# State layer of an encoder block: input weights turned in 64x64 corners, shifted inputs laid by transfers

## The chip, the cores and the metric

The kernel runs on one core of a Trainium2 chip. The metric is the device time of one execution in microseconds (us). Five engines run side by side, each with its own queue worked in order: TensorE (PE in the profile; its weight loads are PEld), VectorE (DVE), ScalarE (ACT), GpSimd (POOL) and SyncE (SP), which here issues nearly all DMA transfers. They wait for each other through semaphores.

## The reference, cut to what matters

One layer of an encoder: 256 tokens of width 2048, all in float32. A normalised input goes through one projection whose columns feed three groups of heads; their outputs are normalised, joined, projected and added to the input; an MLP follows. The change touches the second group, the state layer:

```python
lam_bar = jnp.exp(lam * dt)                       # per group (32) and state (64), complex
b_bar = ((lam_bar - 1.0) / lam)[..., None] * b    # (group, state 64, channel 16)
bu = jnp.einsum('bsgc,gpc->bsgp', u, b_bar)       # what each token puts into each state
a = jnp.broadcast_to(lam_bar, bu.shape)
_, h = lax.associative_scan(combine, (a, bu), axis=1, reverse=reverse)   # x_t = a x_(t-1) + bu_t
y = jnp.einsum('bsgp,gcp->bsgc', h, c).real       # forward and backward, own parameters
```

There are 32 groups of 16 channels, and two directions.

## The kernel before

**The weight stream.** All large weights (209 MB read in all) come as 372 transfers of one stream, `A["w"]`, in the order in which they are used: chunks of 128 x 1024 floats, 512 KB each. `w_dma` issues a chunk on SP into one of three buffers `wraw`. `conv_high` has ACT round it to a shorter format (`wh`), `conv_low` has DVE form the rest (`wl`), three buffers each. `take` hands PE 128 columns at a time; every product is made of three matmuls (high x high, high x low, low x high). When PE comes to chunk c, chunk c + 2 is converted, and after that conversion chunk c + 5 is issued. Chunks 0 to 15 are the first projection columns; 16 to 31 project the memory tokens: a chunk there is 12 matmuls with the weights held (`mem_k`), then 6 with the weights streamed (`mem_v`).

**Tasks between.** All other work is written as Python generators (tasks). `tick`, called twice a chunk, advances them; a rough clock of each engine (`clk`, costs in `Engine.__getattr__`) decides when a task is due. That happens while the program is built: what comes out is one fixed list of instructions per engine. A task's PE work therefore stands at a fixed place among the weight matmuls, and where its inputs are late, all of PE waits.

**The state layer.** Four tokens are taken together as a block (64 blocks, `NB`), 8 groups make a tile `ut` (4 tiles). `prep_b(ut)` has DVE form b_bar times the powers 0 to 3 of lam_bar in `W`, each power from the one before through `pt`. Two groups lie in the 128 partitions of W (states of group j in partitions 64j to 64j + 63). For the products with the inputs, channels have to lie in the partitions: ACT copies W into the zeroed tile `wx`, where group j's 64 columns (4 powers of 16 channels) lie between those of the other group, so that the two don't mix; PE transposes eight 128 x 128 pieces per direction; ACT moves them from PSUM into `W1T`. One `wx` serves both directions in turn.

`U4` holds the layer's input for this: token i of each block in partitions 32i to 32i + 31, so that one matmul sums over four tokens. It is made from `uT` (channels in partitions, blocks along the row) by 16 copies in `g0_evac`, eight each on ACT and POOL. `incr(ut, d)` multiplies: 32 matmuls of 128 rows by 32 columns, four strips of columns of the array side by side. ACT moves the result to `XS`; `tree` scans it on DVE, and `ssm_out` multiplies with c.

In the profile nearly all instructions carry L155, the helper that records an operation, so tiles tell them apart; `U4` is shown as U.

Of the kernel before, what the change touches and what calls it, by code (L numbers as in the profile page):

```python
# [11 lines left out]
F32 = mybir.dt.float32  # L12
# [15 lines left out]
MEMH = 4  # L28
EPS = 1e-6
LAM_RE_MAX = -1e-4  # L30
NB = S // 4
LEV = 6
SCALE = 128 ** -0.5
# [70 lines left out]
def hybrid_kernel(ctx: ExitStack, tc: tile.TileContext, A: dict, out: bass.AP, dbg=None):  # L104
    nc = tc.nc
    ctx.enter_context(tc.manual_schedule())
    mult, add, sub = ALU.mult, ALU.add, ALU.subtract
# [13 lines left out]
    class Engine:  # L121
# [3 lines left out]
        def __getattr__(self, name):  # L125
            f = getattr(self.raw, name)
            e = self.e

            def call(o, *a, **kw):
                n = 1  # L130
                for d in o.shape[1:]:
                    n *= d
                if e == "E":
                    m = a[0].shape[-1]
                    if name == "transpose":
                        c = 110.0
                    elif a[0].dtype == F32R:
                        c = n * 0.4225
                    else:
                        c = max(n, 128) * 1.69 * (0.31 if m == 32 else 1.0) if n > 4 else 110.0  # L140
                elif name == "tensor_reduce":
                    c = 80 + 1.04 * a[0].shape[1] * a[0].shape[2]
                elif e == "A":
                    c = (205 + 0.83 * n + (80 if isinstance(kw.get("scale"), bass.AP) or "bias" in kw else 0)
                         + (186 if "accum_out" in kw else 0))
                elif e == "V":
                    c = (72 if n > 64 else 140) + n * {"tensor_copy": 0.52, "reciprocal": 8.0, "tensor_tensor_scan": 1.04,
                                   "tensor_scalar": 0.76, "memset": 0.3}.get(name, 1.04)
                else:
                    c = 155 + n * {"tensor_scalar": 0.9, "memset": 0.0, "tensor_copy": 1.6}.get(name, 2.1)  # L150
                if e == "V" and n > 64 and name == "tensor_tensor" and any(
                        abs(x.ap[-1][0]) >= 4 for x in (o, a[0]) if x.ap[-1][1] > 1):
                    c += 0.9 * n
                book(e, c)
                return f(o, *a, **kw)  # L155
            return call

    V, G, ACT, PE = (Engine(e, r) for e, r in zip("VGAE", (nc.vector, nc.gpsimd, nc.scalar, nc.tensor)))
# [9 lines left out]
    def att():  # L168
        return ps.tile([128, 512], F32, name="att", tag="bank", bufs=6)
# [4 lines left out]
    def tt(eng, o, a, b, op):  # L174
        eng.tensor_tensor(o, a, b, op=op)
# [10 lines left out]
    def act(o, i, f=AF.Copy, **kw):  # L186
        ACT.activation(o, i, f, **kw)
# [28 lines left out]
    ident = const.tile([128, 128], F32, name="ident")  # L216
# [59 lines left out]
    def after(ns):  # L276
        t = clk["E"] + ns
        while clk["E"] < t:
            yield
# [5 lines left out]
    def done(e):  # L285

        t = clk[e] + MARGIN
        while clk["E"] < t:
            yield
# [11 lines left out]
    class W:  # L301
        raw = {}
# [139 lines left out]
    a2 = A2.enter_context(tc.tile_pool(name="a2", bufs=1, side="right"))  # L442
# [58 lines left out]
    for k in range(KT):  # L501
        c = k if k < 2 else 1 + k // 2
# [149 lines left out]
    W0, CC, XS = {}, {}, {}  # L652
# [5 lines left out]
    uT = a2.tile([128, 4, 256], F32, name="uT")  # L658
    U4 = a2.tile([128, 16, NB], F32, name="U4")

    wx = a2.tile([128, 8, 4, 2, 16], F32, name="wx")
    V.memset(wx.rearrange("p n l j b -> p (n l j b)"), 0.0)

    loaded = {}

    def load_b(ut):
# [5 lines left out]
    def prep_b(ut):  # L672
        yield from until(lambda: ut in loaded and clk["E"] > loaded[ut][1])
        raw = loaded[ut][0]
        w = a2.tile([128, 2, 2, 4, 4, 16], F32, name="W", tag="W", bufs=1)
        par = a2.tile([128, 4, 2, 2, 4], F32, name="par", tag="par", bufs=1)
        for i, x in enumerate((cfr, cfi, lbr, lbi)):
            act(par[:, i], x[:, 8 * ut:8 * ut + 8].rearrange("p (d q) -> p d q", d=2)[:, :, None, :]
                .to_broadcast([128, 2, 2, 4]))
        yield from done("A")  # L680
        for l in range(4):
            o = w[:, :, :, :, l, :]
            src = (w[:, :, :, :, l - 1, :].rearrange("p d c q b -> p (d c q) b") if l
                   else raw.rearrange("p (n b) -> p n b", b=16))
            r_, i_ = (par[:, 2 * min(l, 1) + i].rearrange("p d c q -> p (d c q)")[:, :, None].to_broadcast([128, 16, 16])
                      for i in range(2))
            t = a2.tile([128, 2, 2, 4, 16], F32, name="pt", tag="pt", bufs=1)
            tt(V, t.rearrange("p d c q b -> p (d c q) b"), src, i_, mult)
            tt(V, o.rearrange("p d c q b -> p (d c q) b"), src, r_, mult)
            tt(V, o[:, :, 0], o[:, :, 0], t[:, :, 1], sub)  # L690
            tt(V, o[:, :, 1], o[:, :, 1], t[:, :, 0], add)
            yield True
        yield from done("V")
        act(W0[ut].rearrange("p d c q j b -> p (d c q) j b"),
            w[:, :, :, :, 0, :].rearrange("p d c q b -> p (d c q) b")[:, :, None, :].to_broadcast([128, 16, 2, 16]))
        w0_done.add(ut)
        if ut % 2 == 0:
            XS[ut // 2] = a2.tile([128, 2, 16, NB], F32, name="XS", tag="AB", bufs=2)
        for d in range(2):
            for j in range(2):  # L700
                h = slice(64 * j, 64 * j + 64)
                act(wx[h, :, ::-1 if d == 0 else 1, j, :], w[h, d].rearrange("p c q l b -> p (c q) l b"))
            yield PE
            wt = a2.tile([128, 2, 4, 128], F32, name="W1T", tag="W1T", bufs=2)
            ps2 = [att(), att()]
            for n in range(8):
                PE.transpose(ps2[n // 4][:, n % 4 * 128:(n % 4 + 1) * 128], wx[:, n].rearrange("p l j b -> p (l j b)"),
                             ident)
            for c in range(2):
                act(wt[:, c].rearrange("p q m -> p (q m)"), ps2[c])  # L710
            spawn(incr(ut, d, wt, clk["A"] + MARGIN + LAG[2]), 2, "A")
            yield True

    def incr(ut, d, wt, t0):

        yield from until(lambda: ssm_done and clk["E"] > t0 and (d == 0 or (ut, 0) in xs_part))
        p = att()
        X = p.rearrange("p (c q m) -> p c q m", c=2, q=4)
        for c in range(2):
            for q in range(4):  # L720
                for m in range(4):
                    PE.matmul(X[32 * m:32 * m + 32, c, q, :], wt[:, c, q, 32 * m:32 * m + 32], U4[:, 4 * ut + q, :],
                              start=True, stop=True, skip_group_check=True, tile_position=(0, 32 * m))
        c0 = 8 * (ut % 2) + 4 * d
        act(XS[ut // 2][:, :, c0:c0 + 4, ::-1 if d else 1], X)
        xs_part.add((ut, d))
        yield
# [251 lines left out]
    def g0_evac():  # L979
        b = st_rx["b"]  # L980
        for j in range(2):
            tt(V, qkm[:, 2 * j:2 * j + 2, 0, :], pq[j].rearrange("p (a b) -> p a b", a=2),
               b[:, None, :].to_broadcast([128, 2, 256]), mult)
        yield
        for u in range(4):
            tt(V, uT[:, u].rearrange("p (r c) -> p c r", c=16),
               pu[:, u * 256:(u + 1) * 256].rearrange("p (c r) -> p c r", c=16), b.rearrange("p (c r) -> p c r", c=16),
               mult)
        yield
        for q in range(4):  # L990
            for i in range(4):
                o = U4[32 * i:32 * i + 32, q:16:4, :]
                s = uT[32 * q:32 * q + 32, :, i * NB:(i + 1) * NB]
                if i % 2:
                    G.tensor_copy(o, s)
                else:
                    act(o, s)
            if q < 3:
                yield True
        ssm_done.append(1)  # L1000
        if dbg:
            dbg("uT", uT.rearrange("p a b -> p (a b)"))
        yield
# [64 lines left out]
    for g in range(2):  # L1068
        pv2 = [acc(), acc()]
        for k in range(KT):  # L1070
            wh, wl = take(4)
            for t in range(2):
                s = slice(t * 128, (t + 1) * 128)
# [4 lines left out]
        for h in range(4 * g, 4 * g + 4):  # L1078
            load_bias(h)
            pp = acc()  # L1080
            for j in range(2):
                for k in range(KT):
# [4 lines left out]
                        stop=(k == KT - 1))  # L1087
# [137 lines left out]
    pt = []  # L1225
# [10 lines left out]
    for t, c, _ in parts:  # L1236
        p = acc()
        s = slice(t * 128, (t + 1) * 128)
        b = slice(c.start - 1536, c.stop - 1536)
# [121 lines left out]
    def x1_task():  # L1361
        for o in range(4):
            for t in range(2):
# [8 lines left out]
    rt, r22, r24, vb, v, y, tn, r = (small.tile([128, 2], F32, name=n, bufs=1)  # L1372
                                 for n in ("rt2", "r22", "r24", "vb", "fv", "fy", "ft", "fr2"))
# [28 lines left out]
    for half in range(2):  # L1402
# [19 lines left out]
        for o in range(4):  # L1422
# [18 lines left out]
            c = slice(o * 512, (o + 1) * 512)  # L1441
# [102 lines left out]
```

## Time and profile before

| | us |
|---|---|
| median of 3 runs | 1140.99 (1138.22 to 1141.76) |
| the profiled execution | 1140.01 |
| its span, first to last instruction | 1138.2 |
| PE busy | 1111.2 (98%) |
| DVE busy | 721.3 (63%) |
| ACT busy | 578.3 (51%) |
| POOL busy | 104.8 (9%) |
| mean rate of DMA | 187 GB/s |

Busy time of PE is modelled at the matmuls' ends, so gaps count where they are shown. A row of groups gives the line, the engine, the operation, what is written and read, and the number; a row of a timeline begins with its start and its length in us. A row of stretches gives, after the stretch's length, the busy time of PE, PEld, DVE, ACT and POOL, then the clock granted to TensorE (1.00 is full), the share of the DMA engines and GB/s.

### The profile page before, as it was taken

To read this page: it belongs to the slowest core of one execution; us is meant where nothing else is said; L and a number is where in the kernel's file an instruction comes from. 1 tells how busy PE (TensorE), PEld (TensorE's weight loads), DVE (VectorE), ACT (ScalarE), POOL (GpSimd) and SP (SyncE) were. 2 spreads that over 40 slices of the span, in tenths; PEclk is the share of its full clock that TensorE was granted. 3 is DMA by queue.
4 is the path that set the end of the run, shared out by engine and by line. 5 is a ranking of instruction groups with operands and counts; after the bars stand their busy time and mean duration, and the time that the engine had idled before them with its cause. 6 is when DMAs were issued, how large, how long until landed. Compare 5 with 4: busy or idle time off the path is not lost.

```text
span 1138.2 us, 18307 instructions
## 1 busy us (share of the span) xinstructions
PE 1111.2 (98%) x7208; PEld 957.6 (84%) x7208; DVE 721.3 (63%) x1069; ACT 578.3 (51%) x900; POOL 104.8 (9%) x179
## 2 busy tenths in 40 slices
PE   8999999899999999999999999999999999999996
PEld 8988899799788878888888888888888888888885
DVE  6777588888876776866664444445666665445454
ACT  6567856636655464644455434434444444344341
POOL 1780000020110161000000000000000000001010
PEclk9999999999999999999999999999999999999999
DMA  9876444345455766666666666666666666666663
GB/s 302 291 254 184 127 145 142 114 140 166 135 148 179 249 188 181 189 191 191 187 186 193 189 189 186 186 187 192 193 186 189 191 191 187 186 198 195 193 209 129
DMA packets 62726, 212.31 MB, mean 187 GB/s; under 512 B 7216, under 2 KB 9776, under 8 KB 62640
## 3 DMA queue, kind: packets, MB, share of 16 engines
q1 hardware_dynamic: 62352, 211.05, 60.5%
q8 instruction: 56, 0.92, 0.3%
q14 instruction: 30, 0.25, 0.1%
q10 hardware_dynamic: 288, 0.09, 0.0%
HBM read 209.02 MB, written 2.10 MB: 185 GB/s over the span
## 4 chain that ended last, share of the span: by engine, by line
PE 83%; DVE 7%; DMA 3%; ACT 3%; issue 2%; POOL 1%; SPq 0%; DVEq 0%; POOLq 0%; ACTq 0%
PE acc L155 74%; PE big L155 6%; PE att L155 4%; DMA wraw<-in_w_dram 3%; DVE wl L155 3%; ACT wh L155 1%; DVE ps L155 1%; DVE W L155 1%; DVE XS L155 1%; ACT P L155 0%; DVE pt L155 0%; DVE mn L155 0%; DVE P L155 0%; POOL x L155 0%; DMA gpost<-in_post_dram 0%
## 5 line engine op out<-in xcount | busy, mean ns | idle before, releaser
L155 DVE TENSOR_TENSOR wl<-wraw,wh 128x1024 fp32r<-128x1024 f32 (+1 forms) x372 | 458.3, 1234 | 374.9 <-ACT wh L155 374.3
L155 ACT ACTIVATE wh<-wraw 128x1024 fp32r<-128x1024 f32 (+1 forms) x372 | 391.4, 1054 | 440.5 <-PE acc L155 275.3
L155 PE MATMUL acc<-hs,wh 128*128 128x512 f32 (+1 forms) x996 | 345.9, 391 | 0.0
L155 PE MATMUL acc<-hs,wl 128*128 128x256 f32 x992 | 279.3, 282 | 0.0
L155 PEld LDWEIGHTS acc<-hs,wh 128*128 128x128 f32 x996 | 186.6, 188 | 38.8 <-ACT hs L155 0.2
L155 PEld LDWEIGHTS acc<-hs,wl 128*128 128x128 f32 x992 | 187.3, 189 | 0.0
L155 PE MATMUL acc<-wh,fH 128*128 128x512 f32 x448 | 178.7, 399 | 0.0
L155 PE MATMUL acc<-wh,fL 128*128 128x512 f32 x448 | 176.5, 394 | 0.0
L155 PE MATMUL acc<-wl,fH 128*128 128x512 f32 x448 | 175.7, 392 | 0.0
L155 PEld LDWEIGHTS acc<-wh,fL 128*128 128x128 f32 x448 | 84.1, 188 | 22.0
L155 PEld LDWEIGHTS acc<-wl,fH 128*128 128x128 f32 x448 | 84.1, 188 | 19.9
L155 PEld LDWEIGHTS acc<-wh,fH 128*128 128x128 f32 x448 | 84.1, 188 | 19.4
L155 PE MATMUL acc<-xH,wh 128*128 128x256 f32 x256 | 74.4, 291 | 0.0
L155 PE MATMUL acc<-xH,wl 128*128 128x256 f32 x256 | 72.0, 281 | 1.4 <-DVE wl L155 1.4
L155 PE MATMUL acc<-xL,wh 128*128 128x256 f32 x256 | 71.9, 281 | 0.2 <-issue 0.2
L155 POOL TENSOR_TENSOR facc<-facc,g 128x512 f32<-128x512 f32 x6 | 9.3, 1572 | 474.8 <-DMA g<-in_g_dram 474.8
L155 PEld LDWEIGHTS acc<-xH,wl 128*128 128x128 f32 x256 | 48.3, 188 | 1.9 <-DVE wl L155 1.6
L155 PEld LDWEIGHTS acc<-xH,wh 128*128 128x128 f32 x256 | 48.3, 189 | 0.8
L155 PEld LDWEIGHTS acc<-xL,wh 128*128 128x128 f32 x256 | 48.4, 189 | 0.1
L155 PE MATMUL acc<-wh,mixn 128*128 128x512 f32 x128 | 41.0, 398 | 0.0
L155 ACT ACTIVATE P<-P,mn 128x160 f32<-128x160 f32 (+1 forms) x24 | 10.8, 449 | 46.0 <-DVE mn L155 46.0
L155 DVE TENSOR_TENSOR ps<-XS,pw 128x32 f32<-128x32 f32 (+9 forms) x44 | 30.1, 683 | 1.2
(307 smaller groups left out, 1481.8 us busy)
## 6 DMA issues: line engine op xcount, KB each, us to landing
wraw<-in_w_dram SPq DMA_DIRECT2D x369, 512.0 KB, 3.6
tokst<-in_xt_dram SPq DMA_DIRECT2D x4, 512.0 KB, 7.4
mst<-in_memT_dram SPq DMA_DIRECT2D x4, 512.0 KB, 5.5
tokst<-in_mt_dram SPq DMA_DIRECT2D x4, 512.0 KB, 5.3
x<-in_xt_dram SPq DMA_DIRECT2D x8, 256.0 KB, 5.3
out_dram<-facc SPq DMA_DIRECT2D x8, 256.0 KB, 2.5
xst<-in_xT_dram SPq DMA_DIRECT2D x7, 256.0 KB, 6.4
bias<-in_bias_dram SPq DMA_DIRECT2D x8, 160.0 KB, 3.6
```

The source lines that it names most:

```text
L155: return f(o, *a, **kw)
```

## The change

It has two parts, and costs of the builder's clock that go with them.

1. W is laid out so that for each direction, group pair and part (real or imaginary) the four powers of 16 channels lie in 64 neighbouring columns; the forward direction has them in falling order of power, the backward one in rising order (`power`, with `WSTEP` and `WROW`). `wx`, its zeroing and its copies are gone. Each half of the partitions is turned by itself: a plain matmul of a 64 x 64 piece with the identity, rows and columns 64j to 64j + 63 of the array. Both directions go in one visit. `W1T` is half as wide, and `incr` uses the same two corners: 16 matmuls of 64 x 64 in place of 32 of 128 x 32.
2. `U4` now has group j's tokens together: token i of group j in partitions 64j + 16i to 64j + 16i + 15. This is a shift by 16 partitions, and 32 transfers from SBUF to SBUF on SP make it, 16 partitions x 4 x 64 floats each, in place of the 16 copies. The task then lets 6000 ns of the builder's clock pass before the products may follow.

```diff
-                        c = 110.0
+                        c = 110.0 if n == 128 else 50.0
...
-                        c = max(n, 128) * 1.69 * (0.31 if m == 32 else 1.0) if n > 4 else 110.0
+                        c = max(n, 128) * 1.69 * (0.31 if m == 32 else 1.0 if m > 64 else 0.27) if n > 4 else 110.0
...
-    wx = a2.tile([128, 8, 4, 2, 16], F32, name="wx")
-    V.memset(wx.rearrange("p n l j b -> p (n l j b)"), 0.0)
...
-        w = a2.tile([128, 2, 2, 4, 4, 16], F32, name="W", tag="W", bufs=1)
+        wf = a2.tile([128, WROW], F32, name="W", tag="W", bufs=1)
+        def power(l):
+            a, n = (3 - l) * 16, WSTEP + (2 * l - 3) * 16
+            return (wf[:, a:a + 2 * n].rearrange("p (d x) -> p d x", d=2)[:, :, 0:512]
+                    .rearrange("p d (n l b) -> p d n l b", n=8, l=4)[:, :, :, 0, :])
...
-            tt(V, t.rearrange("p d c q b -> p (d c q) b"), src, i_, mult)
-            tt(V, o.rearrange("p d c q b -> p (d c q) b"), src, r_, mult)
+            tt(V, t, src, i_, mult)
+            tt(V, o, src, r_, mult)
...
-        act(W0[ut].rearrange("p d c q j b -> p (d c q) j b"),
-            w[:, :, :, :, 0, :].rearrange("p d c q b -> p (d c q) b")[:, :, None, :].to_broadcast([128, 16, 2, 16]))
+        for d in range(2):
+            act(W0[ut][:, d].rearrange("p c q j b -> p (c q) j b"),
+                power(0)[:, d][:, :, None, :].to_broadcast([128, 8, 2, 16]))
...
+        yield from done("A")
         for d in range(2):
-            for j in range(2):
-                h = slice(64 * j, 64 * j + 64)
-                act(wx[h, :, ::-1 if d == 0 else 1, j, :], w[h, d].rearrange("p c q l b -> p (c q) l b"))
-            yield PE
-            wt = a2.tile([128, 2, 4, 128], F32, name="W1T", tag="W1T", bufs=2)
-            ps2 = [att(), att()]
+            wt = a2.tile([128, 2, 4, 64], F32, name="W1T", tag="W1T", bufs=2)
+            p = att()
             for n in range(8):
-                PE.transpose(ps2[n // 4][:, n % 4 * 128:(n % 4 + 1) * 128], wx[:, n].rearrange("p l j b -> p (l j b)"),
-                             ident)
-            for c in range(2):
-                act(wt[:, c].rearrange("p q m -> p (q m)"), ps2[c])
+                for j in range(2):
+                    h = slice(64 * j, 64 * j + 64)
+                    PE.matmul(p[h, 64 * n:64 * n + 64], wf[h, WSTEP * d + 64 * n:WSTEP * d + 64 * n + 64], ident[h, h],
+                              start=True, stop=True, skip_group_check=True, tile_position=(64 * j, 64 * j))
+            act(wt.rearrange("p c q m -> p (c q m)"), p)
             spawn(incr(ut, d, wt, clk["A"] + MARGIN + LAG[2]), 2, "A")
...
-                for m in range(4):
-                    PE.matmul(X[32 * m:32 * m + 32, c, q, :], wt[:, c, q, 32 * m:32 * m + 32], U4[:, 4 * ut + q, :],
-                              start=True, stop=True, skip_group_check=True, tile_position=(0, 32 * m))
+                for j in range(2):
+                    h = slice(64 * j, 64 * j + 64)
+                    PE.matmul(X[h, c, q, :], wt[h, c, q, :], U4[h, 4 * ut + q, :], start=True, stop=True,
+                              skip_group_check=True, tile_position=(64 * j, 64 * j))
...
         for q in range(4):
-            for i in range(4):
-                o = U4[32 * i:32 * i + 32, q:16:4, :]
-                s = uT[32 * q:32 * q + 32, :, i * NB:(i + 1) * NB]
-                if i % 2:
-                    G.tensor_copy(o, s)
-                else:
-                    act(o, s)
-            if q < 3:
-                yield True
+            for j in range(2):
+                for i in range(4):
+                    r = 64 * j + 16 * i
+                    nc.sync.dma_start(U4[r:r + 16, q:16:4, :],
+                                      uT[32 * q + 16 * j:32 * q + 16 * j + 16, :, i * NB:(i + 1) * NB])
+        yield from after(6000.0)
         ssm_done.append(1)
```

The lists of instructions show where the moved work stands. Three places follow; each row names the tile written and the tiles read.

PE, where the first product with U4 stands. Before, it comes in the first attention projection (behind chunk 32), with the turning for the next direction behind it:

```order
L155 MATMUL acc<-wh,xL 128x512
L155 MATMUL att<-U_112,W1T 32x64 x32
L155 MATMUL att<-ident,wx 128x128 x8
L155 MATMUL acc<-wh,xH 128x512
L155 MATMUL acc<-wl,xH 128x512
```

With the change, both turnings stand in the middle of chunk 24 of the memory projection, and both products at its end:

```order
L156 MATMUL acc<-memS,wl 128x256
L156 MATMUL att<-ident,W 64x64 x32
L156 MATMUL acc<-wh,memS 128x512
L156 MATMUL acc<-wl,memS 128x512
L156 MATMUL acc<-wh,memS 128x512 x2
L156 MATMUL acc<-wl,memS 128x512
L156 MATMUL acc<-wh,memS 128x512
L156 MATMUL att<-U_112,W1T 64x64 x32
L156 MATMUL acc<-memS,wh 128x256 x2
```

The first product moved forward by eight chunks, and its 16 matmuls together read what all 32 transfers write.

SP, around the 32 transfers. Before (mst is a quarter of the memory tokens, Cw the parameters c, W the parameters b):

```order
L458 DMA mst<-in_memT_dram 128x1024
L319 DMA wraw<-in_w_dram 128x1024 x11
L736 DMA Cw<-in_c_dram 128x256
L319 DMA wraw<-in_w_dram 128x1024 x8
L1066 DMA bias<-in_bias_dram 128x320
```

With the change:

```order
L459 DMA mst<-in_memT_dram 128x1024
L320 DMA wraw<-in_w_dram 128x1024
L1000 DMA U_112<-uT 16x4x64 x32
L320 DMA wraw<-in_w_dram 128x1024 x7
L741 DMA Cw<-in_c_dram 128x256
L320 DMA wraw<-in_w_dram 128x1024 x3
```

The 32 transfers stand between the load of chunk 26 (the one row of wraw behind mst) and that of chunk 27.

PE again, at the last tile's turning. Before, a product and the turning of the other direction stand next to each other:

```order
L155 MATMUL att<-ident,P 128x128 x4
L155 MATMUL att<-U_112,W1T 32x64 x32
L155 MATMUL att<-ident,wx 128x128 x8
L155 MATMUL acc<-wh,xH 128x512
L155 MATMUL acc<-wl,xH 128x512
```

With the change both turnings of that tile come together, and both products after one half of a chunk and some attention work (P, PT, v, qk are the attention's):

```order
L156 MATMUL att<-ident,W 64x64 x32
L156 MATMUL acc<-xH,wh 128x256
L156 MATMUL acc<-xL,wh 128x256
L156 MATMUL acc<-xH,wl 128x256
...
L156 MATMUL att<-PT,v 128x256 x2
L156 MATMUL att<-ident,P 128x128 x4
L156 MATMUL att<-qk 128x160 x2
L156 MATMUL att<-U_112,W1T 64x64 x32
```

No turning is left that reads a copy made by ACT.

More of the change, by code (lines that the diff above doesn't have):

```diff
@@ L30 @@
 LAM_RE_MAX = -1e-4
+WSTEP, WROW = 576, 1248
 NB = S // 4
@@ L681, in prep_b @@
         for l in range(4):
[L682 to L687, printed above, removed]
-            tt(V, t.rearrange("p d c q b -> p (d c q) b"), src, i_, mult)
-            tt(V, o.rearrange("p d c q b -> p (d c q) b"), src, r_, mult)
-            tt(V, o[:, :, 0], o[:, :, 0], t[:, :, 1], sub)
-            tt(V, o[:, :, 1], o[:, :, 1], t[:, :, 0], add)
+            o = power(l)
+            src = power(l - 1) if l else raw.rearrange("p (d n b) -> p d n b", d=2, n=8)
+            r_, i_ = (par[:, 2 * min(l, 1) + i].rearrange("p d c q -> p d (c q)")[:, :, :, None]
+                      .to_broadcast([128, 2, 8, 16]) for i in range(2))
+            t = a2.tile([128, 2, 8, 16], F32, name="pt", tag="pt", bufs=1)
+            tt(V, t, src, i_, mult)
+            tt(V, o, src, r_, mult)
+            tt(V, o[:, :, 0:4], o[:, :, 0:4], t[:, :, 4:8], sub)
+            tt(V, o[:, :, 4:8], o[:, :, 4:8], t[:, :, 0:4], add)
             yield True
         yield from done("V")
-        act(W0[ut].rearrange("p d c q j b -> p (d c q) j b"),
-            w[:, :, :, :, 0, :].rearrange("p d c q b -> p (d c q) b")[:, :, None, :].to_broadcast([128, 16, 2, 16]))
+        for d in range(2):
+            act(W0[ut][:, d].rearrange("p c q j b -> p (c q) j b"),
+                power(0)[:, d][:, :, None, :].to_broadcast([128, 8, 2, 16]))
         w0_done.add(ut)
```

## The prediction

> **What bounds the kernel now.** I began with the page (busy shares, the chain that ended last), then the stretches, then the tiles that the change touches, then SP's queue and TensorE's order of time where the new transfers stand.
>
> ```profile
> span 1138.2 us, 18307 instructions
> PE 1111.2 (98%) x7208; PEld 957.6 (84%) x7208; DVE 721.3 (63%) x1069; ACT 578.3 (51%) x900; POOL 104.8 (9%) x179
> PE 83%; DVE 7%; DMA 3%; ACT 3%; issue 2%; POOL 1%; SPq 0%; DVEq 0%; POOLq 0%; ACTq 0%
> 125.00:150.00 25.00, 24.52 (x328) 21.61 (x327) 14.88 (x21) 17.95 (x35) 0.00 (x0) 1.00 0.48 158
> 150.00:175.00 25.00, 23.62 (x195) 23.31 (x195) 22.57 (x37) 14.72 (x32) 0.97 (x2) 1.00 0.53 158
> 175.00:200.00 25.00, 24.23 (x308) 23.40 (x308) 19.64 (x42) 17.06 (x43) 0.93 (x2) 1.00 0.38 121
> 200.00:225.00 25.00, 21.46 (x216) 17.11 (x215) 19.69 (x36) 15.54 (x32) 1.77 (x3) 0.93 0.37 108
> 275.00:300.00 25.00, 23.93 (x214) 22.74 (x214) 21.94 (x48) 15.98 (x35) 1.35 (x2) 1.00 0.45 132
> 300.00:340.00 40.00, 37.92 (x444) 30.89 (x443) 29.10 (x47) 23.27 (x44) 4.67 (x8) 1.00 0.48 142
> 73.30:110.00 36.70, 36.70 (x290) 32.76 (x291) 28.69 (x56) 29.20 (x45) 9.94 (x19) 1.00 0.65 205
> ```
>
> TensorE sets the end. In a stretch the first figure is its length, the next is PE's busy time. The state layer is worked in, between the weight matmuls, from about 75 to 340 us. In the six stretches from 125 us PE stands still for 0.48 + 1.38 + 0.77 + 3.54 + 1.07 + 2.08 = 9.3 us: this is what a better schedule of the layer could win. From 73.3 to 110 us it has no idle time at all, so whatever newly stops PE there lengthens the run one for one.
>
> **Part 1: the turned weights and their matmuls.**
>
> ```profile
> 108.29 1.10 PE L155 MATMUL att<-U,W1T 128*32 128x64 f32 x64
> 109.32 1.09 PE L155 MATMUL att<-ident,wx 128*128 128x128 f32 x8
> 110.17 0.48 PE L155 MATMUL acc<-wh,xH 128*128 128x512 f32 x1
> L155 PE MATMUL att<-U,W1T x512: 219/219/243, 108.3 to 219.4; 128*32 128x64 f32 x171
> L155 ACT ACTIVATE W1T<-att x16: 572/596/618, 100.9 to 213.4; 128x512 f32<-128x512 f32 x16
> L155 ACT ACTIVATE wx<-W x16: 613/626/630, 94.5 to 210.2; 64x512 f32<-64x512 f32 x16
> ```
>
> For each of 8 (tile, direction) pairs PE now spends 109.32 - 108.29 = 1.03 us on the products and 110.17 - 109.32 = 0.85 us on the turning: 8 x 1.88 = 15.0 us. The 256 product matmuls have 512 records, two each; the 64 transposes have one each. The change makes 16 plain matmuls of both, each 64x64 with 64 moving columns, so 32 + 32 records per pair, 512 in all. The trace has no row for a pair of corners, so bounds. A record with 128 columns takes 0.85/8 = 106 ns of the array, so one with 64 columns 53 ns. If the two corners don't overlap: 512 x 53 ns = 27.1 us, a loss of 12. If they overlap as the four column strips do (1.03/64 = 16 ns a record): 8.2 us, a gain of 7. Two corners at once are 26.5 ns a record, 13.6 us: I take **-1.5 us**, since the four strips show overlap by the number of tiles at a time (four records in 64 ns, near the 53 of one). The dense turning thus saves PE next to nothing: half as many columns, but two records where the transpose had one.
>
> The Trainium skill, "TensorEngine Tiling (Array Packing)", section Restrictions, speaks against this part: column tiling switches off the fp32 transpose mode, so the corners must be turned by ordinary matmuls. The doubled records above say the same; with transpose mode this part would come to half of the turning, about 3.4 us better than I count.
>
> ScalarE is relieved of wx (16 x 0.626 = 10.0 us) and half the W1T evictions (8 x 0.596 = 4.8); W0 costs 4 instructions more. ACT is busy 51%, so that counts only where PE waits for it:
>
> ```profile
> 207.99 1.10 PE L155 MATMUL att<-U,W1T 128*32 128x64 f32 x64
> 210.88 0.66 PE L155 MATMUL att<-ident,wx 128*128 128x128 f32 x4 [1.79 <-ACT wx L155]
> 212.28 1.11 PE L155 MATMUL att<-ident,wx 128*128 128x128 f32 x4 [0.75 <-ACT PT L155]
> PEld att L155 <- ACT wx L155: 2.7, 3, 1.9
> 210.00:212.00 2.00, 0.66 (x4) 0.42 (x4) 0.06 (x1) 1.95 (x4) 0.00 (x0) 1.00 0.00 0
> 212.00:214.00 2.00, 1.72 (x6) 1.57 (x7) 2.00 (x3) 1.77 (x4) 0.00 (x0) 0.52 0.00 0
> 214.00:216.00 2.00, 2.00 (x7) 1.59 (x6) 1.51 (x2) 0.14 (x2) 0.00 (x0) 0.62 0.85 242
> ```
>
> Here the wx copies hold PE (1.79 + 0.75), and then the granted clock falls to 0.52 and 0.62 for 4 us, some 1.7 us of work lost: 4.2 in all. With wx gone both directions are turned from W itself, in one go, so this stall should go; yet each turning still needs its eviction before the product, and the list of instructions sets the later products again only a chunk or so behind. VectorE's work is the same (the scans start some four chunks earlier), so the stalls of 275 to 340 us stay within a few us. I take **-4 us** for the whole schedule; bounds -11 (all 9.3 us and the clock's 1.7) and +2.
>
> **Part 2: the shifted inputs.** Out go eight copies on ACT and eight on POOL, hidden under a full PE. In come 32 transfers of 16 KB on SP, the queue of the weight loads; they stand behind the load of chunk 26 and ahead of that of chunk 27 (a chunk is one transfer of 512 KB).
>
> ```profile
> L155 ACT ACTIVATE U<-uT x8: 396/416/417, 74.4 to 88.0; 32x256 f32<-32x256 f32 x8
> L155 POOL COPY U<-uT x8: 388/398/1281, 76.0 to 83.6; 32x256 f32<-32x256 f32 x8
> 76.75 0.33 SPq L458 DMA_DIRECT2D mst<-in_memT_dram  x1
> 78.08 4.05 SPq L319 DMA_DIRECT2D wraw<-in_w_dram  x3
> DMA to landing us min/median/max: 6.0/6.0/6.0
> 383.70 0.86 SPq L1185 DMA_DIRECT2D x<-in_xt_dram  x2
> 384.61 0.90 SPq L1198 DMA_DIRECT2D gpost<-in_post_dram  x2
> 385.55 0.59 SPq L1185 DMA_DIRECT2D x<-in_xt_dram  x1
> L319 SPq DMA_DIRECT2D wraw<-in_w_dram x372: 327/328/715, 1.2 to 1112.6; - x186
> L1398 SPq DMA_DIRECT2D out_dram<-facc x8: 332/332/348, 1124.2 to 1134.6; - x8
> DMA to landing us min/median/max: 2.3/2.5/2.6
> 82.97 0.40 PE L155 MATMUL acc<-wh,memS 128*128 128x512 f32 x1
> 84.37 0.40 PE L155 MATMUL acc<-memS,wh 128*128 128x256 f32 x2
> L155 ACT ACTIVATE wh<-wraw 128x1024 fp32r<-128x1024 f32 (+1 forms) x372 | 391.4, 1054 | 440.5 <-PE acc L155 275.3
> L155 DVE TENSOR_TENSOR wl<-wraw,wh 128x1024 fp32r<-128x1024 f32 (+1 forms) x372 | 458.3, 1234 | 374.9 <-ACT wh L155 374.3
> wraw<-in_w_dram SPq DMA_DIRECT2D x369, 512.0 KB, 3.6
> ```
>
> *When they are through.* Chunk 26 is issued at 78.08 and takes 0.33, so the train starts at 78.4. Issuing costs at least 0.327 us; queued one behind another, four starts lie (385.55 - 383.70)/4 = 0.46 us apart. In the list of instructions each transfer also waits for the one eight places before it on SP; for the seventh and eighth these are the big loads issued at 76.75 and 78.08, which landed 6.0 us later (the landing row stands for both), at 82.8 and 84.1. So: the eighth at 84.1, 24 more at 0.45 = 94.9, landing like the stores of the end in 2.5: **97.4**. Least: no such wait and 0.37 apart, 78.4 + 31 x 0.37 + 2.3 = 92.2. Most: 84.1 + 24 x 0.53 + 3.6 (a chunk's median landing) = 100.4.
>
> *Who waits.* PE's list now has the first products behind the ninth pair of memory-projection groups (chunk 24), with a wait for all transfers. Before, this point is passed at 84.37, and the first products came at 108.29. The new turning ahead of it adds 1.8 us: PE arrives at 86.2. Queued behind it is every weight matmul; nothing else fills PE. Stall: 97.4 - 86.2 = **+11.2 us**, bounds 6.0 and 14.2. Two or three us of idle PE dropped the clock at 212 us; a stall of this length should too: **+1.7 us**.
>
> *What is late next.* Chunk 27 leaves SP at about 95.4 and not near 80: + 3.6 landing + 1.05 wh + 1.23 wl (the means of its groups) = 101.3. PE first has chunks 25 and 26, 2 x 2.8 us (82.97 to 84.37 is half a chunk), from 97.4 + 0.9: it is there at 103.9. This delay is hidden, by 2.6 us; were PE not stopped, it would stop at chunk 27 instead, so moving the products later on PE alone wouldn't free the path.
>
> **The sum.** The profiled run took 1140.0 us, 1.0 below the median of 1141.0, inside the spread of the three. 1140.0 - 1.5 - 4 + 11.2 + 1.7 = 1147.4; against the median about **1148**.
>
> **The rivals.**
>
> *The layer's stalls outweigh the wait (faster).* All of the 9.3 us of idle PE and the 1.7 us of clock go, and the train runs unhindered: 1140.0 - 1.5 - 11 + 6.0 + 1.7 = 1135. For it: wx is named in the longest stall. Against it: from 275 us on DVE is 88% busy, and its work isn't reduced. It wins once the gains pass the stall. Chance 0.11.
>
> *The train is short (no change).* All SP rows have 128 rows a transfer; one of 16 might be issued faster. At 0.2 us it ends about 84.1 + 24 x 0.2 + 2.5 = 91.4, a stall of 5, no clock drop: 1140.0 + 5 - 5.5 = 1140. Chance 0.15.
>
> *The corners don't overlap (slower still).* Part 1 is +12 in place of -1.5: about 1161. For it: no row has two tiles in different row halves. Against it: the strips overlap fully. Chance 0.10. The Trainium skill, "TensorE: Matmul & The Clock Gate", Part 3, states that tiles at different rows and columns run side by side; no run here shows it yet, and by it this rival falls away.
>
> *The forecast:* 0.64, in itself 1143 to 1154.
>
> A difference under 0.3% (3.4 us) can't be told from none here. The forecast's low end reaches into that by 0.03, so same 0.16, faster 0.12, slower 0.72. A range of 8 in 10 leaves out the far halves of the first and third rivals: 1138 to 1157.
>
> **What would show it.** In the changed profile: 32 transfers U<-uT on SP, 0.4 to 0.5 us apart, from about 78 us; a hole in PE of about 11 us from 86, released by DMA, with a clock near 0.5 for some 3 us behind it; the next chunk load on SP at about 95. From 125 to 340 us PE idle of 5 us rather than 9. PE blocks of 64 records (both directions) of 1.8 us. I am wrong if the first products find their inputs landed, if issuing takes well under 0.3 us, or if the blocks take 3 us.

## The result, and the profile after

The changed kernel takes 1149.76 us (1148.11 to 1150.76, 4 runs) against 1139.76 us (4 runs): ratio 1.0085, 95% interval 1.0061 to 1.0109. The forecast was 1148, with 1138 to 1157 as its range and "slower" at 0.72; the time came out in it.

The first lines of the page after: span, busy times, shares of the chain that ended last.

```profile
span 1149.0 us, 18181 instructions
PE 1113.0 (97%) x7144; PEld 961.2 (84%) x7144; DVE 715.8 (62%) x1068; ACT 563.1 (49%) x872; POOL 104.9 (9%) x171
PE 81%; DVE 6%; DMA 4%; POOL 3%; ACT 2%; issue 2%; SPq 2%; DVEq 0%; POOLq 0%; ACTq 0%
```

PE is busy about as long as before (1111.2). Its idle time grew from 1138.2 - 1111.2 = 27.0 us to 36.0, and SP's queue, 0% of the chain before, has 2%. The stretches after, with the columns as before (length, busy PE, PEld, DVE, ACT, POOL, clock, DMA share, GB/s):

```profile
85.00:90.00 5.00, 2.55 (x24) 1.69 (x20) 1.91 (x3) 2.23 (x8) 0.00 (x0) 1.00 0.10 19
90.00:95.00 5.00, 0.74 (x4) 0.47 (x4) 0.00 (x0) 0.00 (x0) 0.00 (x0) 0.74 0.13 25
95.00:100.00 5.00, 0.88 (x4) 0.57 (x4) 0.00 (x0) 0.00 (x0) 0.00 (x0) 0.50 0.14 26
100.00:105.00 5.00, 2.69 (x44) 2.57 (x46) 0.00 (x0) 0.00 (x0) 0.00 (x0) 0.50 0.53 148
105.00:110.00 5.00, 5.00 (x43) 4.61 (x40) 3.44 (x9) 3.45 (x6) 0.00 (x0) 0.89 0.71 242
125.00:150.00 25.00, 24.67 (x193) 20.17 (x194) 16.42 (x35) 13.94 (x25) 0.18 (x1) 1.00 0.44 130
150.00:175.00 25.00, 24.42 (x287) 21.56 (x286) 22.79 (x32) 16.34 (x32) 0.00 (x0) 1.00 0.55 173
175.00:200.00 25.00, 24.70 (x296) 23.86 (x295) 20.89 (x48) 14.15 (x32) 1.86 (x2) 1.00 0.54 162
200.00:225.00 25.00, 25.00 (x194) 24.33 (x194) 22.74 (x29) 14.23 (x30) 3.15 (x4) 1.00 0.44 134
275.00:300.00 25.00, 24.48 (x229) 23.99 (x228) 21.17 (x38) 14.21 (x31) 1.04 (x2) 1.00 0.57 177
300.00:340.00 40.00, 38.65 (x490) 34.19 (x491) 24.62 (x31) 23.35 (x47) 4.39 (x5) 1.00 0.55 163
```

Two things happened. Between 85 and 105 us PE stands idle for 2.45 + 4.26 + 4.12 + 2.31 = 13.1 us where it was full before, and the clock falls to 0.50 (0.74 is the mean of a stretch in which it falls); DMA moves 19 to 26 GB/s until 100 us, so bandwidth isn't what lacks. In the six stretches behind, which had 9.3 us of idle PE and one clock of 0.93, 0.33 + 0.58 + 0.30 + 0 + 0.52 + 1.35 = 3.1 us are left and the clock stays full. These six were picked where the kernel before stood still; one stretch between them, 250 to 275 us, has 1.2 us of idle PE now where it had 0.2. Over all of 125 to 340 us idle PE fell from 9.5 to 4.3 us (rows further down): the layer's own schedule did gain. The summary of the transfers (length of an issue, least, median and most, in ns; first and last start) and SP's order of time:

```profile
L1000 SPq DMA_DIRECT2D U<-uT x32: 585/593/1758, 78.3 to 100.8; - x32
DMA to landing us min/median/max: 1.8/1.9/6.2
```

```profile
78.32 23.04 SPq L1000 DMA_DIRECT2D U<-uT  x32
101.47 1.47 SPq L320 DMA_DIRECT2D wraw<-in_w_dram  x3
```

The chain of waits has most of the train (the 32 transfers in a row) in it (start, length, what):

```profile
77.93 6.36 DMA wraw<-in_w_dram
84.31 0.59 SPq L1000
84.94 1.76 SPq L1000
86.74 0.59 SPq L1000
...
93.76 0.59 SPq L1000
```

It comes from the landing of chunk 26 at 84.29, which the eighth transfer waits for, and runs on by issues: (93.76 - 86.74)/11 = 0.64 us from one to the next. The last transfer starts at 100.8 and lands some 1.9 us later; chunk 27 leaves SP only at 101.47. PE in order of time, around the hole (start, length; in brackets the idle time ahead and who ended it):

```profile
83.32 2.08 PE L156 MATMUL att<-ident,W 64*64 64x64 f32 x64
85.33 0.50 PE L156 MATMUL acc<-wh,memS 128*128 128x512 f32 x1
...
86.93 0.33 PE L156 MATMUL att<-U,W1T 64*64 64x64 f32 x2
87.65 0.30 PE L156 MATMUL att<-U,W1T 64*64 64x64 f32 x2 [0.40 <-DMA U<-uT]
90.09 0.29 PE L156 MATMUL att<-U,W1T 64*64 64x64 f32 x2 [2.14 <-DMA U<-uT]
...
102.75 3.00 PE L156 MATMUL att<-U,W1T 64*64 64x64 f32 x50 [2.00 <-DMA U<-uT]
105.69 0.68 PE L156 MATMUL acc<-memS,wh 128*128 128x256 f32 x2
```

PE reaches the products at 86.93, gets on by two records whenever their four transfers have landed, is free at 102.75 and through at 105.69.

### The profile page after: what moved, and what is told of

It is laid out like the page before. It is cut to its first block, busy times and chain, and to the rows that moved or that the text cites. A ratio compares the mean times of both kernels' runs of the same rounds, so it can differ in the third digit from the quotient of the medians.

```text
span 1149.0 us, 18181 instructions
## 1 busy us (share of the span) xinstructions
PE 1113.0 (97%) x7144; PEld 961.2 (84%) x7144; DVE 715.8 (62%) x1068; ACT 563.1 (49%) x872; POOL 104.9 (9%) x171
## 4 chain that ended last, share of the span: by engine, by line
PE 81%; DVE 6%; DMA 4%; POOL 3%; ACT 2%; issue 2%; SPq 2%; DVEq 0%; POOLq 0%; ACTq 0%
PE acc L156 72%; PE big L156 5%; PE att L156 4%; DMA wraw<-in_w_dram 3%; DVE wl L156 3%; SPq L1000 1%; ACT wh L156 1%; DVE W L156 1%; POOL u L156 1%; DVE pt L156 0%; POOL acc L156 0%; POOL cs L156 0%; DVE ps L156 0%; DMA gpost<-in_post_dram 0%; POOL x L156 0%
## 5 line engine op out<-in xcount | busy, mean ns | idle before, releaser
L156 PEld LDWEIGHTS acc<-wh,fL 128*128 128x128 f32 x448 | 84.1, 188 | 21.9
L156 PEld LDWEIGHTS acc<-wh,fH 128*128 128x128 f32 x448 | 84.1, 188 | 19.4
L156 DVE TENSOR_TENSOR XS<-XS,ps 128x32 f32<-128x32 f32 (+9 forms) x44 | 30.0, 682 | 1.1
```

## The experiments

Ratios are against the kernel before, timed on the same chip beside each run.

**The train alone.** The kernel before, with 32 transfers of the same kind on SP into a buffer that nobody reads; everything else, PE's order too, stays.

```diff
+        U5 = a2.tile([128, 2, 16, NB], F32, name="U5", tag="AB", bufs=2)[:, 0]
+        for q in range(4):
+            for j in range(2):
+                for i in range(4):
+                    r = 64 * j + 16 * i
+                    nc.sync.dma_start(U5[r:r + 16, q:16:4, :],
+                                      uT[32 * q + 16 * j:32 * q + 16 * j + 16, :, i * NB:(i + 1) * NB])
```

> The kernel before, with its copies and its order on TensorE untouched, and 32 more transfers of 16 x 4 x 64 floats on SP at the place where the change has them, into a buffer that nothing reads. Theory (the train holds back the weight loads behind it): the train ends on SP near 101.4 us as in the changed kernel, chunk 27 is converted by 107.7 and TensorE wants it at 89.9, so TensorE stops there for some 17 us and the clock falls; 1139.8 + 17 + 2 = 1159. Rival (only the products' wait for the inputs costs, the weights are buffered far enough ahead): 1140, no stop.

Measured: 1157.32 us, ratio 1.0147 (1.0132 to 1.0162). The theory gave 1159. Its SP row of the transfers with the one behind it, and the PE row with the long wait:

```profile
77.32 21.81 SPq L995 DMA_DIRECT2D U<-uT  x32
99.23 10.53 SPq L319 DMA_DIRECT2D wraw<-in_w_dram  x6
```

```profile
104.32 0.80 PE L155 MATMUL acc<-memS,wh 128*128 128x256 f32 x2 [14.06 <-ACT wh L155]
```

Nobody waits for these transfers, and yet PE stands for 14.06 us: chunk 27 could not be issued before 99.23. The train costs 16.5 us though nobody reads it. Whether the cause is its place in SP's queue or its traffic, the runs on POOL's queue below tell apart.

**The corners alone.** The changed kernel with the 16 old copies on ACT and POOL in place of the transfers. The regrouping of the inputs is left out with them.

```diff
-            for j in range(2):
-                for i in range(4):
-                    r = 64 * j + 16 * i
-                    nc.sync.dma_start(U4[r:r + 16, q:16:4, :],
-                                      uT[32 * q + 16 * j:32 * q + 16 * j + 16, :, i * NB:(i + 1) * NB])
-        yield from after(6000.0)
+            for i in range(4):
+                o = U4[32 * i:32 * i + 32, q:16:4, :]
+                s = uT[32 * q:32 * q + 32, :, i * NB:(i + 1) * NB]
+                if i % 2:
+                    G.tensor_copy(o, s)
+                else:
+                    act(o, s)
+            if q < 3:
+                yield True
```

> The changed kernel with the 16 copies of the kernel before in place of the 32 transfers. The copies lay the inputs in the old arrangement, so the products mix other channels than they should: the regrouping of the inputs is left out, everything else is done. Theory (the corners are worth the stalls that they remove, some 7 us of the 10 to 17 between the two traces, at no cost on TensorE): 1132 to 1134. Rival (the corners bring nothing, and the changed kernel lost only some 10 us to the transfers): 1139 to 1141.

Measured: 1129.92 us, ratio 0.9906 (0.9891 to 0.9921). That is below both expectations. Its row of busy times, and three of its stretches:

```profile
PE 1108.6 (98%) x7144; PEld 958.1 (85%) x7144; DVE 717.2 (64%) x1068; ACT 566.5 (50%) x880; POOL 105.0 (9%) x179
```

```profile
200.00:225.00 25.00, 25.00 (x255) 21.04 (x254) 23.18 (x26) 12.71 (x31) 5.67 (x6) 1.00 0.46 148
275.00:300.00 25.00, 24.37 (x303) 22.52 (x302) 23.73 (x29) 13.18 (x28) 2.29 (x4) 1.00 0.57 173
300.00:340.00 40.00, 40.00 (x316) 32.90 (x316) 22.91 (x40) 25.00 (x42) 3.78 (x6) 1.00 0.49 148
```

The corners are worth 10.9 us, twice the forecast's 1.5 + 4. The span fell by 1138.2 - 1127.7 = 10.5; idle time of PE went from 27.0 to 19.1 us (-7.9), busy time from 1111.2 to 1108.6 (-2.6; the clock, 0.93 in 200 to 225 us before, stays at 1.00). The stalls of 300 to 340 us are gone, for which the prediction saw DVE as the limit: DVE has 22.91 us there, not 29.10, and more of its work earlier (23.18 us from 200 to 225, where it had 19.69). Part of them moved: from 250 to 275 us PE is idle for 1.5 us, 0.2 before.

**The products later.** The changed kernel, with the products let in later by the builder's clock, behind the landing of the train. All else stays.

```diff
-        yield from after(6000.0)
+        yield from after(24000.0)
```

> The changed kernel with 24000 in place of 6000 ns between the transfers and the products in the builder's clock: the first products then stand behind chunk 29, past the landing. Theory (the prediction's remark that the weight loads behind the train would stop TensorE instead): TensorE stops at chunk 27 for some 15 us, 1147 to 1151, as the changed kernel. Rival (the wait of the products is the whole cost): 1132 to 1135.

Measured: 1145.54 us, ratio 1.0044 (1.0027 to 1.0061). Its rows of SP, then of PE:

```profile
77.16 22.23 SPq L1000 DMA_DIRECT2D U<-uT  x32
99.50 0.52 SPq L320 DMA_DIRECT2D wraw<-in_w_dram  x1
```

```profile
104.51 0.79 PE L156 MATMUL acc<-memS,wh 128*128 128x256 f32 x2 [11.99 <-ACT wh L156]
```

The wait for the products is gone; PE stops 11.99 us for chunk 27 instead, where the theory had some 15, and the time lies 1.5 us below its range. Only 4 us are won.

**The transfers on POOL's queue**, first with the products later, then with the products where the change has them. The whole computation is done in both.

```diff
-                    nc.sync.dma_start(U4[r:r + 16, q:16:4, :],
+                    nc.gpsimd.dma_start(U4[r:r + 16, q:16:4, :],
```

> As the run with the products later, with the 32 transfers issued on POOL's queue, which is idle there. Theory (SP's queue being taken is what costs): the weight loads flow, TensorE has no stop before chunk 29; if POOL issues one transfer in under 0.7 us the inputs have landed by then and the time is 1132 to 1135; at 1 us each the train ends near 109 and TensorE waits some 10 us for it, 1143. Rival (transfers within SBUF slow the weight loads themselves): 1140 or more with late landings of the chunks.

> The changed kernel, its 32 transfers issued on POOL's queue instead of SP's, and the products left where the change put them (behind chunk 24 of the memory projection); nothing is left out. With the run that has both the other queue and the later products (1127.2 us) and the one that has the later products alone (1145.5 us) this fills the square of queue and place. Theory, there are two waits of which the later one sets the end, the products' wait for the 32nd transfer and the weight projection's wait for chunk 27: on POOL the last transfer was issued at 96.7 us and landed about 4 us later, so the products still stop PE from 87 to about 98 to 101 us, with the clock falling to half; the weights now come in time, and the time is 1143 to 1149 us. Rival, the queue of the weights is the whole cause: with SP free the time is within 3 us of the run with both, 1125 to 1131 us.

| | products behind chunk 24 | products later |
|---|---|---|
| train on SP | 1149.76 us, 1.0085 (1.0061 to 1.0109) | 1145.54 us, 1.0044 (1.0027 to 1.0061) |
| train on POOL | 1144.21 us, 1.0032 (1.0020 to 1.0043) | 1127.20 us, 0.9890 (0.9872 to 0.9907) |

On POOL with the products later (the profiled execution took 1130.66 us): its busy times, its transfers, and PE's first products.

```profile
PE 1109.0 (98%) x7144; PEld 959.0 (85%) x7144; DVE 715.5 (63%) x1068; ACT 562.6 (50%) x872; POOL 117.8 (10%) x203
```

```profile
L1000 POOL DMA_DIRECT2D U<-uT x32: 512/512/746, 77.7 to 96.7; - x32
DMA to landing us min/median/max: 1.6/4.0/5.9
```

```profile
104.39 2.08 PE L156 MATMUL att<-U,W1T 64*64 64x64 f32 x64
```

On POOL with the products early, PE's first products, and the last that waited:

```profile
87.52 0.33 PE L156 MATMUL att<-U,W1T 64*64 64x64 f32 x4
...
97.08 3.00 PE L156 MATMUL att<-U,W1T 64*64 64x64 f32 x50 [1.34 <-DMA U<-uT]
```

Neither change does much by itself, both together win some 22 us over the changed kernel and beat the kernel before by 1.1%. Two waits lie side by side, products for transfers and weights for SP; taking one away uncovers the other. With both gone the 64 records run through in 2.08 us without a bracket, and the time is below the 1132 to 1135 us expected. The rival that transfers within SBUF slow the weight loads falls with the same run: the transfers are all made there, and from 75 to 340 us PE waits for weights nowhere over 0.4 us. With the products early, 1144.21 us lies in the range of the theory of two waits.

The Trainium skill, "DMA: Bandwidth & Descriptors", section "Issuing engines are not separate DMA queues", says that issuing from several engines saves only the sequencer's time to start a DMA, "which is usually small relative to the DMA itself". The first half fits the runs: from POOL's queue the same transfers cost SP no time. The second half falls short here: an issue took 0.59 us of the 1.9 us to the landing, and the 32, with waits for two big loads among them, held SP for 23.04 us, with the next weight load behind them.

**Spread out on SP.** The changed kernel, transfers on SP, given out by twos between the weight loads; the turned weights get four buffers in place of two.

```diff
-            wt = a2.tile([128, 2, 4, 64], F32, name="W1T", tag="W1T", bufs=2)
+            wt = a2.tile([128, 2, 4, 64], F32, name="W1T", tag="W1T", bufs=4)
...
+        n = 0
...
                     nc.sync.dma_start(U4[r:r + 16, q:16:4, :],
                                       uT[32 * q + 16 * j:32 * q + 16 * j + 16, :, i * NB:(i + 1) * NB])
+                    n += 1
+                    if n % 2 == 0:
+                        yield
```

> The changed kernel with its 32 transfers still on SP, but given out by twos, a step of the projection between two pairs, and so woven between the loads of chunks 27 to 38; the products move behind that, and four W1T buffers hold the turned weights until then. Theory, what costs is that 24 transfers in a row stand ahead of one weight load: two or four transfers ahead of each load delay it by 1.3 to 2.6 us, which the loads' lead covers nearly everywhere, so the time is 1126 to 1134 us, like the run on POOL's queue. Rival, SP's time is what lacks: the same 32 x 0.64 = 20 us of issuing delay the loads all the same, PE starves a little at many chunks, and the time stays at 1140 us or more.

Measured: 1139.01 us, ratio 0.9992 (0.9982 to 1.0001): neither expectation, 1 us below the rival's. PE's rows around the products:

```profile
113.22 1.50 PE L156 MATMUL att<-U,W1T 64*64 64x64 f32 x12 [1.34 <-ACT BD L156]
115.31 0.30 PE L156 MATMUL att<-U,W1T 64*64 64x64 f32 x2 [0.58 <-DMA U<-uT]
117.93 6.11 PE L156 MATMUL att<-U,W1T 64*64 64x64 f32 x114 [2.33 <-DMA U<-uT]
```

The loads come in time now: from 99 us up to the products PE waits nowhere over 0.25 us for weights. But the last transfer starts only at 116.0, and the products, whose place in PE's list comes at 113.2, wait for it until 117.93; the 114 records behind the wait then take 6.11 us where 114 x 31 ns would be 3.6, at a lowered clock (0.67 and 0.64 in the stretches from 115 and 120 us). The theory was right on the loads and wrong on where the products would stand.

**What makes an issue 0.59 us long.** Three kernels like the train alone (each edit stands for itself; the lines show where it differs from the train alone, the second has its own loop), with other idle transfers of 16 KB at the same place: one run of 1 KB a partition instead of four pieces; all 128 partitions with 128 bytes each; and 16 partitions of 1 KB read from device memory.

```diff
-                    nc.sync.dma_start(U5[r:r + 16, q:16:4, :],
-                                      uT[32 * q + 16 * j:32 * q + 16 * j + 16, :, i * NB:(i + 1) * NB])
+                    nc.sync.dma_start(U5[r:r + 16, 4 * q:4 * q + 4, :],
+                                      uT[32 * q + 16 * j:32 * q + 16 * j + 16, i, :].rearrange("p (a b) -> p a b", a=4))
...
+        for n in range(32):
+            nc.sync.dma_start(U5[:, n // 2, 32 * (n % 2):32 * (n % 2) + 32],
+                              uT[:, n // 8, 32 * (n % 8):32 * (n % 8) + 32])
...
+                    nc.sync.dma_start(U5[r:r + 16, 4 * q:4 * q + 4, :],
+                                      A["xt"][32 * q + 16 * j:32 * q + 16 * j + 16, 0, i * 256:(i + 1) * 256].rearrange("p (a b) -> p a b", a=4))
```

> The kernel before plus 32 idle transfers on SP, as in the run with the train alone (1157.3 us), but each of the 16 partitions now gets one run of 1 KB in place of four pieces of 256 bytes; the same bytes from the same tile at the same place of the queue. Theory, the pieces make the issue long (0.59 us in place of 0.33 to 0.43): the starts of the transfers stand 0.40 to 0.48 us apart, the next chunk leaves SP 4 to 5 us earlier than with the pieces (99.2 us there), and the time is 1151 to 1154 us. Rival, it is the kind of transfer (within SBUF, or 16 partitions) and not its pieces: still 0.6 us apart, and 1156 to 1158 us.

> The kernel before plus 32 idle transfers on SP at the same place, again within SBUF and again of 16 KB, but each over all 128 partitions (128 bytes a partition) instead of 16 partitions (1 KB a partition). The pieces are ruled out as what makes the issue 0.59 us long (0.587 us with one piece a partition). Theory, it is the 16 partitions: over 128 partitions the issue takes 0.33 to 0.43 us like the other rows of SP, the starts stand 0.37 to 0.48 us apart, chunk 27 leaves SP 4 to 6 us earlier than with the one-piece rows (100.5 us there) and the time is 1152 to 1155 us. Rival, it is the way from SBUF to SBUF, whatever the shape: 0.59 us, 0.63 apart, and 1156 to 1160 us.

> The kernel before plus 32 idle transfers on SP at the same place, of 16 partitions and 1 KB a partition as in the one-piece rows, but read from device memory (the input xt) instead of SBUF. Theory of the 16 partitions: issue 0.59 us, 0.63 us apart, 1156 to 1160 us. Rival, the way from SBUF to SBUF is what is long: issue 0.33 to 0.43 us, 0.37 to 0.48 apart, and 1152 to 1155 us.

Measured: 1159.03 us, ratio 1.0157 (1.0140 to 1.0174); 1157.93 us, 1.0146 (1.0129 to 1.0163); 1154.67 us, 1.0118 (1.0103 to 1.0134). In all three the rival came true, in the first with a time 1 us above its range. The summaries of the three, in this order:

```profile
L995 SPq DMA_DIRECT2D U<-uT x32: 507/587/1028, 79.2 to 99.8; - x32
```

```profile
L992 SPq DMA_DIRECT2D U<-uT x32: 465/599/1547, 78.5 to 100.6; - x32
```

```profile
L995 SPq DMA_DIRECT2D U<-in_xt_dram x32: 310/418/1138, 77.8 to 95.2; - x32
```

Neither the pieces nor the number of partitions matters: 0.587 and 0.599 us. Read from device memory, the same 16 rows of 1 KB take 0.418. In these kernels it is the way from SBUF to SBUF that costs 0.17 us more an issue. Why, no run shows.

## Why the prediction was right, point by point

Against the profiled execution of before (1140.01 us) that of after took 1150.76, so +10.75; the forecast's terms were -1.5 - 4 + 11.2 + 1.7 = +7.4.

- **Who waits, and for what: right.** The start of the train (78.32; forecast 78.4), the waits of the seventh and eighth transfer for the landing of big loads (the eighth was issued at 84.31; forecast 84.1) and PE's arrival (86.93; forecast 86.2) came as worked out.
- **The pitch of the train: mis-sized most.** "24 more at 0.45" took (100.8 - 84.31)/24 = 0.69 us each: 0.64 as a rule, and one issue of 1.76 us. The 0.45 was read from rows with device memory on one side, where it holds: the run from device memory has (95.2 - 77.8)/31 = 0.56 with its early waits, and an issue of 0.418. The landing was shorter (1.9, not 2.5). The release came at 102.75, not 97.4, beyond the bound of 100.4.
- **Stall and clock.** The block of products took 105.69 - 86.93 = 18.8 us; undisturbed it is 85.33 - 83.32 = 2.0 for the same 64 records (the turning; in the run on POOL the products too). So the wait and the low clock cost 16.7 us, 13.1 of them idle, where 11.2 + 1.7 = 12.9 were forecast.
- **The corners' own time.** Eight blocks of 2.01 us are 16.1 us against 15.0: +1.1, not -1.5. A record takes 2.01/64 = 31 ns where 26.5 were assumed and 53 would be no overlap; the rival of corners one after the other falls. The Trainium skill, "TensorE: Matmul & The Clock Gate", Part 3, has tiles at different rows and columns run concurrently; the 31 ns agree. A pair of corners takes 63 ns, as long as four strips did (64). The prediction read the doubled records as a sign that a corner can't use the transpose mode; they show only that these plain float32 matmuls have two records each (64 for the 32 of a turning), and no run tries that mode in a corner.
- **The schedule: too small, inside its bounds.** What is left of +10.75 after 16.7 and 1.1 is -7.1, where -4 was taken out of -11 to +2. It is a remainder, but rows bear it out: from 125 to 340 us idle PE fell from 9.5 to 4.3 us, about as the prediction's sign had it (9 and 5), and the 1.7 us of low clock at 212 us went too, 6.9 in all. The -4 had only the stall at the wx copies in it. That stall went, as said; others between 125 and 250 us shrank with it (6.2 us of idle PE there in all before, 1.2 after). From 250 to 340 us about as much was left (3.4 and 3.1), but not for the reason given: DVE "88% busy" holds from 275 to 300 us alone (29.10 of 40 us behind it are 73%), and with the products later hardly any idle PE is left (0.2 us from 125 to 340) although DVE has as much work in all (715.1 us, 715.8 in the changed kernel). With the corners alone the term is -10.9 - 1.1 = -12, just beyond the -11 of the first rival, which lost because the wait was larger still.
- **"It would stop at chunk 27 instead": right.** The train alone (14.06 us for wh) and the later products (11.99 us for wh) show it. In the changed kernel itself chunk 27 was hidden, as forecast.

The three errors, +3.8, +2.6 and -3.1, partly cancel; the sum is 3.3 us above the forecast's. That it came so close is in part luck; that the time went up, and by which wait, is not. The rival of a short train fell the other way: an issue of these transfers isn't shorter but longer, and by the way from SBUF to SBUF, not by the 16 rows.

By the ratios train and corners together would be 16.5 - 10.9 = +5.6, and the changed kernel is at +9.7. The stretch from 125 to 340 us shows where part of the rest lies (columns as before; the kernel before, the change, the corners alone, the products later, POOL's queue with the products early, POOL's queue with the products later):

```profile
125.00:340.00 215.00, 205.45 (x2338) 185.84 (x2337) 171.17 (x293) 130.00 (x262) 16.70 (x25) 0.99 0.47 142
125.00:340.00 215.00, 210.70 (x2270) 191.70 (x2271) 172.58 (x287) 123.82 (x246) 17.54 (x23) 1.00 0.50 151
125.00:340.00 215.00, 212.89 (x2192) 193.66 (x2191) 177.24 (x302) 124.83 (x247) 17.25 (x25) 1.00 0.49 150
125.00:340.00 215.00, 214.78 (x2303) 195.57 (x2299) 173.79 (x285) 129.35 (x263) 19.92 (x26) 1.00 0.49 148
125.00:340.00 215.00, 211.33 (x2186) 191.64 (x2185) 173.56 (x286) 125.87 (x249) 18.43 (x26) 1.00 0.48 148
125.00:340.00 215.00, 214.93 (x2207) 195.55 (x2206) 178.08 (x299) 124.00 (x246) 19.68 (x26) 1.00 0.51 154
```

Idle PE is 9.5, 4.3, 2.1, 0.2, 3.7 and 0.1 us. With the products early it is about the same on either queue, with the products later next to nothing on either: what the layer's schedule gains goes with the place of the products, not with the queue. So some 3.6 us of what the later products win on POOL's queue are stalls far behind the train, and 2.2 of the 4.1 us that the changed kernel lacks against the sum lie here (4.3 - 2.1). Each row is one profile; why the later place fits the weights better, and where the rest lies, was not taken apart.

## What to carry to other kernels

Count a transfer first by the time for which its issue holds the queue, and by who stands behind it there: 32 small transfers ahead of one weight load cost 16 us with no byte of bandwidth short. Before moving a wait, look for the second one that the same work causes; here queue and place of the consumer had to move together. A change that loses as a whole can hold a part that wins: time the parts apart.

## What the hardware showed beyond expectation

- Issuing a transfer of 16 KB on SP took 0.59 to 0.60 us from SBUF to SBUF, in three shapes, and 0.42 us from device memory to SBUF; on POOL's queue 0.51 us.
- In each of the six trains on SP one issue took 1.0 to 1.8 us, in the spread-out run two; on POOL's queue none took over 0.75. No row names a cause.
- PE's clock fell to 0.50 although PE woke for two records about every 2.5 us. The Trainium skill, "TensorE: Matmul & The Clock Gate", Part 1, puts half rate after an idle window of about 3.4 us; here no gap was longer than 2.2 us, and visits of 0.3 to 0.45 us did not keep the clock up.
- Two 64 x 64 corners in float32 with 64 columns run at 31 ns a record, 63 ns a pair.
